# The first adaLN modulation of a two-layer diffusion block: plain fp32 weights in four column groups instead of split weights

## The chip, the cores and the metric

The kernel runs on one core of a Trainium2 chip. The metric is the device time of one execution in microseconds (us), as the median of several runs; lower is better. All tensors in HBM are fp32.

## The reference, cut to what matters

Two layers run over 256 latent tokens and 256 context tokens of width 1024. Every layer begins by turning the conditioning vectors `c` (latent) and `c_ctx` (context) into six modulation vectors each, and the first two of these shift and scale the normalised input of the token mixer:

```python
silu_c, silu_cc = jax.nn.silu(c), jax.nn.silu(c_ctx)
mod_lat = (silu_c @ w_mod[l] + b_mod[l])[:, None, :]      # w_mod[l]: 1024 x 6144
mod_ctx = silu_cc @ w_mod[l] + b_mod[l]
sh1, sc1, gt1, sh2, sc2, gt2 = jnp.split(mod_lat, 6, axis=-1)
h  = rms_norm(x,   g_pre_mix[l]) * (1.0 + sc1)  + sh1
hc = rms_norm(ctx, g_pre_mix[l]) * (1.0 + csc1) + csh1
... = jnp.split(h @ w_in[l], SPLIT_POINTS, axis=-1)       # w_in[l]: 1024 x 6912
```

The case is about the very first of these products, `sh1` and `sc1` of layer 0 for both streams, because nothing else can start on TensorE in earnest before them: `h` is needed by every later product of the layer.

## The kernel before, in words

Almost all products of the kernel are "split" products. A helper (`split`, L163; in the prologue `cut`, L252) writes a fp32 tile as the sum of two fp32r tiles, a high part (a cast on ScalarE) and a low part (a subtraction on VectorE). `mm3` (L178) then adds up three TensorE products: high by high, high by low, low by high. `mm3_pair` (L184) does the same for two independent products whose operands sit in different halves of the partitions, and issues the two alternately. Weights come from HBM in tiles of 512 KB (128 partitions x 1024 fp32).

**The prologue** (L233 to L355) computes `sh1` and `sc1` of layer 0, modulates the input, and does the first 512 columns of `w_in` (the retention's q and k). It works in four rounds `kp` of 256 channels. A round needs five weight tiles: four of `w_mod` (two vectors, and two halves `hf` of the contraction over 1024; each tile holds four blocks `k` of 128 rows, 256 columns wide) and one of `w_in`. The steps of a round have one letter each in `PLAN` (L54):

- `c`: `cut` up to tile n: high part on ScalarE, low part on VectorE. `cut` also calls `load`, so a transfer is issued on SP only `PLD` = 4 tiles ahead of the cutting.
- `a`: `mod` (L275): the stationary operand is `msr` (128 columns of which four are not zero: high and low part of silu(c) and of silu(c_ctx)), the moving operands are the high and the low weight tile. That makes 4 tiles x 4 blocks x 2 parts = 32 products of 256 columns, all into one PSUM tile `modps`.
- `r`: `row` (L286): ScalarE copies the four useful rows into `r5`, whose fifth row is the bias, brought by a transfer of its own (`bias`, L289).
- `t`: `pre_tr` (L500): TensorE transposes of the normalised input, eight of 128 columns for both streams, into `ph`.
- `f`: `fin` (L294): four plain fp32 products with a 5x2 selector turn the rows into columns `sh1`, `sc1` (PSUM tile `pm`, then three small VectorE instructions).
- `h`: `pre_h` (L509): four ScalarE instructions make h of both streams and two blocks of 128 channels, and VectorE splits each into `hT` (a cast and a subtraction).
- `g`: `gemm` (L306): 24 products of 512 columns into the four PSUM tiles `pr`.

While `Ordered.on` is true, VectorE, ScalarE and TensorE instructions keep the order of the program. Other instructions (transfers on POOL, splits of later weights, `setup2`) are put between them by the scheduler of the framework. `tc.issue_after(ins)` makes the instructions of a block follow `ins` on that instruction's own engine only. The last `gemm(3)` is issued after `Ordered.on` has been cleared.

Ahead of the prologue stands `setup` (L1264). Behind it `setup2` (L1275) brings the rope tables, the retention's decays and the gains by transfers on POOL, and computes decays on VectorE; it follows the last low part (`st["hold"]`) on VectorE. The following steps are the retention's v (`projB`, PSUM tile `pB`) and then the remaining projections, whose weights (`wr`, split into `wh` and `wl`) use three buffers each. The rest of the modulation is done on VectorE (`mod_dve`, L391) from `w_mod` rows that POOL brings (`mr`). The neighbourhood attention brings its bias tiles `bt` on POOL (L796).

The buffers: `sp` has `NS` = 31 tiles of 4 KB per partition (`S(...)`), used for X, weight tiles, `hT` and so on; `wrp`, `whp`, `wlp` have three each; PSUM has four banks `mm` and four banks `at`.

Of the kernel before, what the change touches and what calls it, by code (L numbers as in the profile page):

```python
# [9 lines left out]
F32 = mybir.dt.float32  # L10
# [23 lines left out]
C1 = 0  # L34
# [46 lines left out]
def kernel(  # L81
# [115 lines left out]
    cs = const.tile([128, 8, 2], F32, tag="cs", name="cs")  # L197
    brow = const.tile([128, 2, 512], F32, tag="brow", name="brow")
# [34 lines left out]
    def prologue():  # L233
        pr = []
        M = {}
        raw, rdy = {}, {}
# [3 lines left out]
        mi = (0, 5, 10, 15)  # L240
        gi = (4, 9, 14, 19)

        def load(n):
            while len(raw) < min(n, len(wts)):
                i = len(raw)
                ap, k, _, _ = wts[i]
                t = S("pr", F32) if i % RW else wrp.tile([128, 2, 512], F32, tag="wr", name="pr")
                raw[i] = t
                st["hold_sp"] = nc.sync.dma_start(
                    out=t.rearrange("p a b -> p (a b)").rearrange("p (k n) -> p k n", k=k), in_=ap)  # L250

        def cut(n):  # L252
            while len(rdy) < min(n, len(wts)):
# [7 lines left out]
                rdy[i] = [u.rearrange("p a b -> p (a b)").rearrange("p (k n) -> p k n", k=k) for u in (hi, lo)]  # L261

        def init():
            msr = S("msr")
            v_.tensor_copy(msr[:, 0, :], brow[:, 0, :])
            v_.tensor_copy(msr[:, 1, :], brow[:, 0, :])
            msr = msr.rearrange("p a b -> p (a b)").rearrange("p (k m) -> p k m", k=8)
            v_.tensor_copy(msr[:, :, 0:2], cs)
            tt(msr[:, :, 2:4], cs, f(msr[:, :, 0:2]), ALU.subtract)
            M["msr"] = msr  # L270
# [18 lines left out]
        def bias(kp):  # L289
            r5 = st["r5", kp] = T("r5")  # L290
            nc.gpsimd.dma_start(out=r5[4:5, :].rearrange("o (v n) -> o v n", v=2),
                                in_=b_mod[0:1, 0:2 * D].rearrange("o (v n) -> o v n", v=2)[:, :, 256 * kp:256 * kp + 256])

        def fin(kp):  # L294
            r5 = st.pop(("r5", kp))
# [10 lines left out]
        def gemm(kp):  # L306
            w_ = rdy[gi[kp]]
# [6 lines left out]
        def go(ws):  # L314
            Ordered.on = True
            load_x(4)
            load(PLD)
            for kp in range(2):
                bias(kp)
# [4 lines left out]
            cut(C1)  # L324
            pre_xn(1, sq[1])
            for kp, plan in enumerate(PLAN):
                for c in plan.replace("_", " ").split():
                    o, n = c[0], int(c[1:])
                    if o == "c":
                        cut(n)  # L330
                    elif o == "a":
                        mod(n)
                    elif o == "r":
                        row(n)
                    elif o == "t":
                        ph = [pre_tr(n, s) for s in range(2)]
                    elif o == "f":
                        fin(n)
                        if n < 2:
                            bias(n + 2)  # L340
                    elif o == "h":
                        h32 = [T("h32") for _ in range(2)]
                        for j in range(2):
                            for s in range(2):
                                pre_h(0, 0, n, s, ph[s], (j,), h32[s])
# [1147 lines left out]
```

## Time and profile before

| | us |
|---|---|
| runs (device time) | 1476.2, 1478.07, 1477.75 |
| median | 1477.75 |
| the profiled execution's own time | 1477.88 |
| its span on the core (first to last instruction) | 1476.1 |
| time around the span | 1.78 |

The profile names instructions by engine (PE is TensorE's matmul, PEld its weight load, DVE is VectorE, ACT is ScalarE, POOL is GpSimd, SP is the sync engine whose queue issues most transfers), by line and by the names of the tiles written and read. Because of the `Ordered` wrapper almost every compute instruction has line 72, so the tile names tell them apart. A row of a timeline merges equal neighbours; its first number is the start in us from the beginning of the span, its second the length, and the bracket at the end tells how long the engine had been idle and what it had waited for. Matmul records overlap, because a record includes the pipeline's fill and drain; the pace is read from the start of one to the start of the next, or from a piece of the chain divided by its count.

### The profile page before, as it was taken

What the parts mean: (1) busy time and instruction counts of PE and PEld (TensorE: products, weight loads), DVE (VectorE), ACT (ScalarE), POOL (GpSimd) and SP (SyncE); (2) the same over time, 40 slices, a digit from 0 to 9 for tenths busy, and PEclk for the clock granted to TensorE, in tenths of its full rate; (3) what the DMA queues carried; (4) which work ended last, traced back from release to release, by engine and by line L of the source; (5) the groups of instructions that cost most, each with busy time, mean ns of one, the idle gap of its engine ahead of it and who ended that gap; (6) DMA issues with size and microseconds to landing.
All of it is one profiled execution on the core that took longest, in us unless ns stands there. A gap on an engine that the chain in (4) does not pass through costs nothing.

```text
span 1476.1 us, 20910 instructions
## 1 busy us (share of the span) xinstructions
PE 1427.8 (97%) x7926; PEld 1210.6 (82%) x7926; DVE 1079.2 (73%) x1999; ACT 746.6 (51%) x1259; POOL 68.1 (5%) x131
## 2 busy tenths in 40 slices
PE   4999999999999999999999999999999999799997
PEld 3878788877788888988878887788889999699886
DVE  5785687777998759977756546986877887667544
ACT  5563465555333447724335145664556665477542
POOL 2000000000110000100001101000000000000000
PEclk9999899999999999999999999999999999899999
DMA  8622122222566555746447547443223446378653
GB/s 290 193 73 72 43 58 71 63 87 80 167 178 188 166 199 172 239 148 213 157 129 228 169 130 242 145 129 101 72 86 106 145 140 187 113 210 251 209 185 116
DMA packets 231958, 219.64 MB, mean 149 GB/s; under 512 B 7653, under 2 KB 188957, under 8 KB 231857
## 3 DMA queue, kind: packets, MB, share of 16 engines
q1 hardware_dynamic: 217856, 170.42, 37.7%
q0 software_dynamic: 14000, 47.88, 10.7%
q8 instruction: 62, 1.02, 0.3%
q14 instruction: 40, 0.32, 0.1%
HBM read 217.22 MB, written 1.05 MB: 148 GB/s over the span
## 4 chain that ended last, share of the span: by engine, by line
PE 78%; issue 12%; DMA 4%; DVE 4%; ACT 1%; SPq 0%; POOL 0%; DVEq 0%; ACTq 0%; POOLq 0%
PE ps L72 33%; PE pO L72 20%; PE pB L72 6%; PE br L72 5%; DMA mr<-in_w_mod_dram 2%; PE po L72 2%; PE pt L72 2%; PE pr L72 2%; PE sl L72 2%; PE gkv L72 1%; PE modps L72 1%; DMA pr<-in_w_mod_dram 1%; PE ro L72 1%; DVE wl L72 1%; DVE acc L72 1%
## 5 line engine op out<-in xcount | busy, mean ns | idle before, releaser
L72 PE MATMUL ps<-hT,wh 128*128 128x256 f32 (+1 forms) x2480 | 602.5, 334 | 1.5 <-ACT wh L72 1.5
L72 ACT CAST wh<-wr 128x1024 fp32r<-128x1024 f32 x295 | 309.5, 1052 | 443.7 <-PE pO L72 175.9
L72 DVE TENSOR_TENSOR wl<-wr,wh 128x1024 fp32r<-128x1024 f32 x295 | 359.4, 1221 | 206.2 <-ACT wh L72 205.6
L72 PEld LDWEIGHTS ps<-hT,wh 128*128 128x128 f32 x2480 | 417.4, 189 | 54.5 <-issue 6.9
L72 PE MATMUL ps<-hT,wl 128*128 128x256 f32 (+1 forms) x1240 | 413.3, 333 | 2.2 <-DVE wl L72 2.2
L72 PEld LDWEIGHTS ps<-hT,wl 128*128 128x128 f32 x1240 | 233.8, 189 | 26.5 <-DVE wl L72 3.5
L72 PE MATMUL pO<-wh,u 128*128 128x512 f32 x768 | 243.4, 396 | 0.0
L72 PEld LDWEIGHTS pO<-wh,u 128*128 128x128 f32 x768 | 144.2, 188 | 34.7
L72 DVE SCALAR_TENSOR_TENSOR acc<-mr,cs,acc 128x1024 f32<-128x1024 f32 x112 | 141.1, 1280 | 30.1 <-DMA mr<-in_w_mod_dram 29.5
L72 PE MATMUL pO<-wl,u 128*128 128x512 f32 x384 | 152.0, 396 | 1.2 <-DVE wl L72 1.2
L72 PEld LDWEIGHTS pO<-wl,u 128*128 128x128 f32 x384 | 72.1, 188 | 18.9 <-DVE wl L72 1.6
L72 PE MATMUL pB<-wh,hT 128*128 128x512 f32 x256 | 83.6, 396 | 0.0
L448 POOL DMA_DIRECT2D mr<-in_w_mod_dram x80 | 43.0, 537 | 647.6 <-DVE acc L72 609.6
L72 PE MATMUL pO<-wh,yT 128*128 128x512 f32 x192 | 60.7, 395 | 0.0
L72 PEld LDWEIGHTS pB<-wh,hT 128*128 128x128 f32 x256 | 48.0, 187 | 11.2
L72 DVE TENSOR_TENSOR PT<-pt,PT 128x512 fp32r<-128x512 f32 x80 | 51.4, 681 | 2.9 <-ACT PT L72 2.3
L72 PE MATMUL pB<-wl,hT 128*128 128x512 f32 x128 | 50.5, 394 | 0.0
L72 ACT CAST PT<-pt 128x512 fp32r<-128x512 f32 x80 | 43.2, 600 | 8.6 <-PE pt L72 6.7
L72 PEld LDWEIGHTS pO<-wh,yT 128*128 128x128 f32 x192 | 35.9, 188 | 8.6
L72 PE MATMUL pt<-ident,P 128*128 128x128 f32 x320 | 42.0, 273 | 0.7 <-DVE P L72 0.5
L72 DVE TENSOR_TENSOR u<-rl,u 128x256 fp32r<-128x256 f32 (+1 forms) x71 | 36.6, 516 | 7.6 <-ACT u L72 7.5
L72 DVE TENSOR_SCALAR P<-P,su 128x512 f32<-128x512 f32 (+1 forms) x96 | 40.2, 439 | 1.6
(261 smaller groups left out, 1901.9 us busy)
## 6 DMA issues: line engine op xcount, KB each, us to landing
wr<-in_w_m_dram SPq DMA_DIRECT2D x143, 512.0 KB, 4.6
wr<-in_w_in_dram SPq DMA_DIRECT2D x104, 512.0 KB, 3.8
mr<-in_w_mod_dram POOLq DMA_DIRECT2D x80, 512.0 KB, 4.5
wr<-in_w_br_dram SPq DMA_DIRECT2D x24, 512.0 KB, 3.5
wr<-in_w_out_dram SPq DMA_DIRECT2D x24, 512.0 KB, 4.1
pr<-in_w_mod_dram SPq DMA_DIRECT2D x16, 512.0 KB, 7.0
bt<-in_relb_dram POOLq DMA_DIRECT2D x16, 192.0 KB, 2.8
X<-in_x_dram SPq DMA_DIRECT2D x4, 512.0 KB, 5.2
```

The source lines that it names most:

```text
L72: ins = call(*a, **k)
L448: nc.gpsimd.dma_start(out=w, in_=w_mod[l, 128 * kc:128 * kc + 128, vec * D:vec * D + D].rearrange("p (a n) -> p a n", a=2))
```

## The change

The four weight tiles of `w_mod` of a round are no longer split. Their fp32 tiles are moving operands as they come from HBM. The stationary operand is `csz`: for each of the eight blocks of the contraction 32 columns, of which two hold silu(c) and silu(c_ctx) in plain fp32 and thirty are zero. Block `k` of a tile writes the 32 PSUM partitions `32k` to `32k+31`, so four partial sums stand side by side; only `hf` accumulates. `row` is now a VectorE addition of the PSUM tile and a bias tile that is zero but for rows 0 and 1, and `fin` multiplies all 128 rows with a 128x2 selector `selp` that adds the four groups. Only the four `w_in` tiles are still split, by `cast` (`c`, ScalarE) and `cut` (`d`, VectorE). All 20 loads are issued at once (17 into `sp` tiles, three into `wrp`). When the 15th (`GATE` = 14) has landed, a small POOL copy into `late` runs; the transfers of `setup2`, `mr` and `bt` follow that copy on POOL. The list of the steps is new.

```diff
-C1 = 0
-RW = 2
-PLD = 4
-PLAN = ["c4 t0 a0 c5 r0 f0 h0 c9 g0 c13",
-        "a1 t1 r1 c14 f1 h1 c18",
-        "a2 r2 c19 g1 t2 f2 h2",
-        "a3 t3 r3 c20 f3 h3 g2"]
+PLAN = "t0 a0 c0 r0 f0 d0 h0 g0 a1 r1 t1 c1 f1 d1 h1 a2 r2 t2 g1 c2 f2 d2 h2 a3 r3 t3 g2 c3 f3 d3 h3"
+GATE = 14
...
-        def load(n):
-            while len(raw) < min(n, len(wts)):
-                i = len(raw)
-                ap, k, _, _ = wts[i]
-                t = S("pr", F32) if i % RW else wrp.tile([128, 2, 512], F32, tag="wr", name="pr")
+        def load():
+            for i, (ap, k, _, _) in enumerate(wts):
+                t = wrp.tile([128, 2, 512], F32, tag="wr", name="pr") if i % 5 == 4 and i < 15 else S("pr", F32)
                 raw[i] = t
-                st["hold_sp"] = nc.sync.dma_start(
-                    out=t.rearrange("p a b -> p (a b)").rearrange("p (k n) -> p k n", k=k), in_=ap)
-
-        def cut(n):
-            while len(rdy) < min(n, len(wts)):
-                i = len(rdy)
-                load(i + PLD)
-                t, k = raw[i], wts[i][1]
-                hi = whp.tile([128, 2, 512], F32R, tag="wh", name="pwh") if i % 3 == 0 else S("pwh")
-                lo = wlp.tile([128, 2, 512], F32R, tag="wl", name="pwl") if i % 3 == 0 else S("pwl")
-                st["hold_act"] = s_.copy(hi, t)
-                st["hold"] = tt(lo, t, f(hi), ALU.subtract)
...
+                st["hold_sp"] = nc.sync.dma_start(out=flat(t, k), in_=ap)
+                if i == GATE:
+
+                    st["late"] = nc.gpsimd.tensor_copy(out=late, in_=t[:, 0, 0:1])
+
+        def cast(kp):
+            hi[kp] = whp.tile([128, 2, 512], F32R, tag="wh", name="pwh")
+            st["hold_act"] = s_.copy(hi[kp], raw[5 * kp + 4])
+
+        def cut(kp):
+            lo = wlp.tile([128, 2, 512], F32R, tag="wl", name="pwl")
+            st["hold"] = tt(lo, raw[5 * kp + 4], f(hi[kp]), ALU.subtract)
+            rdy[kp] = [flat(u, 2) for u in (hi[kp], lo)]

         def init():
...
+            M["bias"] = [S("bias", F32) for _ in range(2)]
+            for i, t in enumerate(M["bias"]):
+                v_.memset(t, 0.0)
+                for kp in range(2):
+                    c = 512 * i + 256 * kp
+                    nc.gpsimd.dma_start(
+                        out=t[0:2, kp, :].rearrange("o (v n) -> o v n", v=2),
+                        in_=b_mod[0, 0:2 * D].partition_broadcast(2).rearrange("o (v n) -> o v n", v=2)[:, :, c:c + 256])
+            v_.memset(selp, 0.0)
+            for j in range(4):
+                r = slice(32 * j, 32 * j + 2)
+                v_.tensor_copy(selp[r, :], ident[r, r])
...
         def mod(kp):
-            ps = att("modps")
+            ps = M["ps", kp] = att("modps")
             for i in range(4):
                 v, hf = i // 2, i % 2
-                w = rdy[mi[kp] + i]
+                w = flat(raw[5 * kp + i], 4)
                 for k in range(4):
-                    for p in range(2):
-                        t_.matmul(ps[:, 256 * v:256 * v + 256], M["msr"][:, 4 * hf + k, :], w[p][:, k, :],
-                                  start=(hf == 0 and k == 0 and p == 0), stop=(hf == 1 and k == 3 and p == 1))
-            M["ps", kp] = ps
+                    t_.matmul(ps[32 * k:32 * k + 32, 256 * v:256 * v + 256], csz[:, 4 * hf + k, :], w[:, k, :],
+                              start=(hf == 0), stop=(hf == 1))

         def row(kp):
-            s_.copy(st["r5", kp][0:4, :], M["ps", kp][0:4, :])
...
+            r = M["r", kp] = T("r5")
+            tt(r, M["ps", kp], M["bias"][kp // 2][:, kp % 2, :], ALU.add)
...
-                t_.matmul(pt[:, 2 * j:2 * j + 2], r5[0:5, 128 * j:128 * j + 128], sel[0:5, 18:20],
-                          start=True, stop=True)
+                t_.matmul(pt[:, 2 * j:2 * j + 2], r[:, 128 * j:128 * j + 128], selp, start=True, stop=True)
...
             gemm(3)
-            with tc.issue_after(st["hold"].ins):
+            with tc.issue_after(st["hold"].ins), tc.issue_after(st["late"].ins):
                 setup2()
...
-                nc.gpsimd.dma_start(
-                    out=w, in_=w_mod[l, 128 * kc:128 * kc + 128, vec * D:vec * D + D].rearrange("p (a n) -> p a n", a=2))
...
+                with tc.issue_after(st["late"].ins):
+                    nc.gpsimd.dma_start(
+                        out=w, in_=w_mod[l, 128 * kc:128 * kc + 128, vec * D:vec * D + D].rearrange("p (a n) -> p a n", a=2))
...
-                        nc.gpsimd.dma_start(out=bt, in_=relb[l, h])
+                        with tc.issue_after(st["late"].ins):
+                            nc.gpsimd.dma_start(out=bt, in_=relb[l, h])
...
+        v_.memset(csz, 0.0)
+        v_.tensor_copy(csz[:, :, 0:2], cs)
```

## Rows read from the trace of the kernel before

**Rows 1.** The page: TensorE's share, and the chain that ended last by engine.

```profile
PE 1427.8 (97%) x7926; PEld 1210.6 (82%) x7926; DVE 1079.2 (73%) x1999; ACT 746.6 (51%) x1259; POOL 68.1 (5%) x131
...
PE 78%; issue 12%; DMA 4%; DVE 4%; ACT 1%; SPq 0%; POOL 0%; DVEq 0%; ACTq 0%; POOLq 0%
```

**Rows 2.** Windows: us, busy PE, PEld, DVE, ACT, POOL, granted clock, DMA share, GB/s.

```profile
4.00:16.00 12.00, 1.38 (x4) 0.68 (x4) 5.41 (x33) 5.64 (x9) 6.37 (x12) 1.00 1.02 336
...
31.00:36.00 5.00, 5.00 (x12) 3.86 (x13) 4.93 (x9) 5.00 (x7) 0.00 (x0) 0.50 0.45 154
...
40.00:74.00 34.00, 34.00 (x215) 30.31 (x214) 25.48 (x74) 18.67 (x30) 1.01 (x2) 1.00 0.56 175
```

**Rows 3.** The chain in order of time, 0 to 76 us: start, length, what.

```profile
4.13 16.13 DMA pr<-in_w_mod_dram
...
22.64 4.57 PE modps L72 x23
...
27.86 1.06 PE pm L72 x8
...
30.82 8.37 PE pr L72 x24
39.19 3.78 PE modps L72 x32
42.97 0.87 PE ph L72 x8
43.84 0.98 PE pm L72 x8
...
48.80 5.51 PE pr L72 x24
...
61.96 11.12 PE pr L72 x48
```

**Rows 4.** ScalarE's timeline: its waits for transfers, 8 to 26 us.

```profile
8.65 1.06 ACT L72 ACTIVATE xj<-X 128x1024 f32<-128x1024 f32 x1 [0.28 <-DMA X<-in_xc_dram]
...
12.75 1.06 ACT L72 ACTIVATE xj<-X 128x1024 f32<-128x1024 f32 x1 [2.95 <-DMA X<-in_xc_dram]
...
20.28 1.04 ACT L72 CAST pwh<-pr 128x1024 fp32r<-128x1024 f32 x1 [4.85 <-DMA pr<-in_w_mod_dram]
...
24.66 1.05 ACT L72 CAST pwh<-pr 128x1024 fp32r<-128x1024 f32 x1 [0.34 <-DMA pr<-in_w_in_dram]
```

**Rows 5.** POOL's timeline: issues of `setup2`, `mr`, and a wait.

```profile
4.60 0.55 POOL L1276 DMA_DIRECT2D lgt<-in_decay_dram  x1
...
12.06 0.54 POOL L448 DMA_DIRECT2D mr<-in_w_mod_dram  x1 [1.00 <-DMA lgt<-in_decay_dram]
...
63.96 0.50 POOL L451 DMA_DIRECT2D brow<-in_b_mod_dram  x1 [50.63 <-DVE lgp L72]
64.49 0.50 POOL L1282 DMA_DIRECT2D sel<-in_sel_dram  x1
```

**Rows 6.** Groups by tile and shape, 0 to 75 us: busy us, mean ns.

```profile
L72 DVE TENSOR_TENSOR pwl<-pr,pwh 128x1024 fp32r<-128x1024 f32 x20 | 23.5, 1219 | 8.6 <-ACT pwh L72 8.6
...
L72 PE MATMUL pm<-sel,r 5*128 5x2 f32 x32 | 4.2, 249 | 0.7 <-ACT r L72 0.7
```

**Rows 7.** VectorE's timeline: rows at 8.4, 13.9, 29.0 and 94.8 us.

```profile
8.41 0.17 DVE L72 TENSOR_SCALAR pv<-pms 128x2 f32<-128x2 f32 x1 [4.09 <-ACT xj L72]
...
13.93 0.17 DVE L72 TENSOR_SCALAR pv<-pms 128x2 f32<-128x2 f32 x1 [2.33 <-ACT xj L72]
...
28.95 0.16 DVE L72 COPY sh<-pm 128x4 f32<-128x4 f32 x1 [1.98 <-PE pm L72]
...
94.75 0.69 DVE L72 TENSOR_TENSOR rv<-pB,rv 128x512 fp32r<-128x512 f32 x1 [0.71 <-ACT rv L72]
```

**Rows 8.** TensorE's timeline: the first product of the modulation.

```profile
17.73 0.56 PE L72 MATMUL modps<-pwh,msr 128*128 128x256 f32 x1
```

**Rows 9.** TensorE's timeline, 101.0 to 101.8 us: a pair of row halves.

```profile
101.02 0.98 PE L72 MATMUL ra<-rq,rk 64*128 64x256 f32 x12
```

More of the change, by code (lines that the diff above doesn't have):

```diff
@@ L197 @@
     cs = const.tile([128, 8, 2], F32, tag="cs", name="cs")
+    csz = const.tile([128, 8, 32], F32, tag="csz", name="csz")
+    selp = const.tile([128, 2], F32, tag="selp", name="selp")
+    late = const.tile([128, 1], F32, tag="late", name="late")
     brow = const.tile([128, 2, 512], F32, tag="brow", name="brow")
@@ L235, in prologue @@
         M = {}
-        raw, rdy = {}, {}
+        raw, hi, rdy = {}, {}, {}
         md = lambda kp: [wspec(w_mod[0], 512 * hf, 4, v * D + 256 * kp, 256) for v in range(2) for hf in range(2)]
@@ L252, in cut @@
-        def cut(n):
-            while len(rdy) < min(n, len(wts)):
-                i = len(rdy)
-                load(i + PLD)
-                t, k = raw[i], wts[i][1]
-                hi = whp.tile([128, 2, 512], F32R, tag="wh", name="pwh") if i % 3 == 0 else S("pwh")
-                lo = wlp.tile([128, 2, 512], F32R, tag="wl", name="pwl") if i % 3 == 0 else S("pwl")
-                st["hold_act"] = s_.copy(hi, t)
-                st["hold"] = tt(lo, t, f(hi), ALU.subtract)
-                rdy[i] = [u.rearrange("p a b -> p (a b)").rearrange("p (k n) -> p k n", k=k) for u in (hi, lo)]
@@ L263, in init @@
-        def init():
[L264 to L270, printed above, removed]
+        flat = lambda t, k: t.rearrange("p a b -> p (a b)").rearrange("p (k n) -> p k n", k=k)
+        def load():
+            for i, (ap, k, _, _) in enumerate(wts):
+                t = wrp.tile([128, 2, 512], F32, tag="wr", name="pr") if i % 5 == 4 and i < 15 else S("pr", F32)
+                raw[i] = t
+                st["hold_sp"] = nc.sync.dma_start(out=flat(t, k), in_=ap)
+                if i == GATE:
+                    st["late"] = nc.gpsimd.tensor_copy(out=late, in_=t[:, 0, 0:1])
@@ L275, in mod @@
         def mod(kp):
-            ps = att("modps")
+            ps = M["ps", kp] = att("modps")
             for i in range(4):
                 v, hf = i // 2, i % 2
-                w = rdy[mi[kp] + i]
+                w = flat(raw[5 * kp + i], 4)
                 for k in range(4):
-                    for p in range(2):
-                        t_.matmul(ps[:, 256 * v:256 * v + 256], M["msr"][:, 4 * hf + k, :], w[p][:, k, :],
-                                  start=(hf == 0 and k == 0 and p == 0), stop=(hf == 1 and k == 3 and p == 1))
-            M["ps", kp] = ps
+                    t_.matmul(ps[32 * k:32 * k + 32, 256 * v:256 * v + 256], csz[:, 4 * hf + k, :], w[:, k, :],
+                              start=(hf == 0), stop=(hf == 1))
         def row(kp):
-            s_.copy(st["r5", kp][0:4, :], M["ps", kp][0:4, :])
[L289 to L292, printed above, removed]
+            r = M["r", kp] = T("r5")
+            tt(r, M["ps", kp], M["bias"][kp // 2][:, kp % 2, :], ALU.add)
         def fin(kp):
-            r5 = st.pop(("r5", kp))
+            r = M.pop(("r", kp))
             pt = att("pm")
             for j in range(4):
-                t_.matmul(pt[:, 2 * j:2 * j + 2], r5[0:5, 128 * j:128 * j + 128], sel[0:5, 18:20],
-                          start=True, stop=True)
+                t_.matmul(pt[:, 2 * j:2 * j + 2], r[:, 128 * j:128 * j + 128], selp, start=True, stop=True)
             p3 = pt[:, 0:8].rearrange("p (j e) -> p j e", e=2)
@@ L306, in gemm @@
         def gemm(kp):
-            w_ = rdy[gi[kp]]
+            w_ = rdy[kp]
             for k in range(2):
@@ L316, in go @@
             load_x(4)
-            load(PLD)
-            for kp in range(2):
-                bias(kp)
+            load()
             init()
@@ L323, in go @@
             sq.append(pre_sq(1))
-            cut(C1)
             pre_xn(1, sq[1])
[L326 to L345, printed above, removed]
-                    elif o == "g":
-                        gemm(n)
+            ph = {}
+            for c in PLAN.split():
+                o, n = c[0], int(c[1:])
+                if o == "c":
+                    cast(n)
+                elif o == "d":
+                    cut(n)
+                elif o == "a":
+                    mod(n)
+                elif o == "r":
+                    row(n)
+                elif o == "t":
+                    ph[n] = [pre_tr(n, s) for s in range(2)]
+                elif o == "f":
+                    fin(n)
+                elif o == "h":
+                    h32 = [T("h32") for _ in range(2)]
+                    for j in range(2):
+                        for s in range(2):
+                            pre_h(0, 0, n, s, ph[n][s], (j,), h32[s])
+                elif o == "g":
+                    gemm(n)
             Ordered.on = False
             gemm(3)
-            with tc.issue_after(st["hold"].ins):
+            with tc.issue_after(st["hold"].ins), tc.issue_after(st["late"].ins):
                 setup2()
@@ L447, in go @@
                 w = mrp.tile([128, 2, 512], F32, tag="mr", name="mr")
-                nc.gpsimd.dma_start(
-                    out=w, in_=w_mod[l, 128 * kc:128 * kc + 128, vec * D:vec * D + D].rearrange("p (a n) -> p a n", a=2))
-                if kc == 0:
-                    nc.gpsimd.dma_start(out=brow[0:1], in_=b_mod[l:l + 1, vec * D:vec * D + D].rearrange("o (a n) -> o a n", a=2))
+                with tc.issue_after(st["late"].ins):
+                    nc.gpsimd.dma_start(
+                        out=w, in_=w_mod[l, 128 * kc:128 * kc + 128, vec * D:vec * D + D].rearrange("p (a n) -> p a n", a=2))
+                    if kc == 0:
+                        nc.gpsimd.dma_start(out=brow[0:1], in_=b_mod[l:l + 1, vec * D:vec * D + D].rearrange("o (a n) -> o a n", a=2))
                 for s in streams:
```

2 lines of the change are left out of this document (removed).

## The prediction

> **What bounds the kernel now.** I read the page first: TensorE has work on it for 97% of the span and holds 78% of the chain that ended last [rows 1]. A change is therefore worth what it does to TensorE's own sequence: it shortens it, or it removes a wait in it. The change touches only the prologue, so I went on to the windows of the first 74 us [rows 2]. There are two stages. Up to about 26 us the transfers rule: TensorE works 1.4 of 12 us between 4 and 16 us while the DMA engines are full (share 1.02, 336 GB/s). From 31 us on TensorE is busy in every microsecond of the windows shown. The chain in order of time says the same [rows 3]: one transfer of w_mod until 20.26, then `modps` to 27.21, the finish of round 0, and from 30.82 to 73.08 matmul pieces with no gap. So what counts is when the first of the four `gemm` pieces starts (30.82), what stands on TensorE from there to 73.08, and whether a new gap appears.
>
> Two further readings. First, the pace. At full clock the 32 products of 256 columns take 3.78 us, 0.118 each, and 24 of 512 columns 5.51 us, 0.23 each [rows 3]. Between 31 and 36 us the granted clock is 0.50, that is 1.2 instead of 2.4 GHz, and 12 products take 5 us [rows 2]; TensorE had waited 1.9 us before [rows 3]. The 23 products from 22.64 on took 4.57 us, which is about 18 at half pace and five at full pace: the clock rose near 26.3, after some 3.7 us of these products. Second, the transfers. Weight tiles land one after another: three steps from 20.28 to 24.66, 1.46 us each [rows 4]. But the fourth X tile came 4.1 us after the third [rows 4], because POOL's transfers ran then [rows 5].
>
> **The change, part by part.** *Removed:* 16 of the 20 splits, each a cast on ScalarE and 1.22 us on VectorE [rows 6], and 128 products of 256 columns. After 31 us the splits lie beside gapless matmuls, so there their removal is worth nothing. In round 0 it is worth something, as part of an earlier start:
>
> - X. Without POOL's transfers beside it the fourth X tile lands one step after the third: 8.65 + 1.46 = 10.1 instead of 12.75. The statistics of the context stream then could start at 11.3 (13.93 is 1.18 behind 12.75), but the latent stream's, from 8.41, hold VectorE about 3.2 us (13.93 to 17.73 less 0.6 of transposes) [rows 7, 8]; so 11.65, which is 2.3 us earlier. TensorE is through with the transposes at 17.73 - 2.3 = 15.4.
> - The weights. The four tiles of round 0 follow X directly: 10.1 + 4 x 1.46 = 15.9, instead of 23.2 (one step before 24.66) [rows 4]. The 15th lands at 32, the 20th at 39 if nothing else runs; POOL's 1.9 MB behind the gate (the sizes of those tensors) add at most 6 us at 336 GB/s. Round 3 wants them after 50, so the gate itself costs and gains nothing; without that cover it would be those 6 us. The loads wait for no buffer: 4 X, 17 weight and 2 bias tiles leave 8 of 31, as many as `hT` needs.
>
> *Added, the new products:* 16 per round. Plain fp32 products leave two records each (32 `pm` records for 16 products in the code) [rows 6], so a round has 32 records of 256 columns. No row shows what such a record costs over many columns. Lower end: 0.118, one stream of 256 columns. Upper end: 0.228, the row of 512 columns, if it streams its columns twice. I take 0.228: `mm3` needs three split products and still drops low by low, so two records that keep all four must hold two each. A page of the Trainium skill, FP8 and Floating Point Precision, TensorE Precision Notes, states four passes for true fp32; a product would by it cost four times 0.118, an estimate of 0.47 that moves the sum by 0.4 us.
>
> *How far the four groups overlap.* No row shows column groups; the nearest is the pair of row halves: twelve products of 256 columns within 0.98 us [rows 9], where one after another would be 12 x 0.118 + 0.16 = 1.58. So products in different parts of the array do run side by side, and there the code issues the halves alternately. In `mod` it does not: the two records of a product are neighbours in the same 32 columns. If starts keep the program's order, the second record waits for the first, and the next group can start only beside the second. Then two of four groups overlap, and 16 products take 17 steps of 0.228 = 3.9 us, against 3.8 now. Ends: 1.8 us (all four side by side) and 7.3 (none).
>
> The Trainium skill bears on this: TensorE: Matmul & The Clock Gate, Part 3, says that matmuls start and end in program order and only weight loads move ahead. By that rule the sum is the one above; by its own table for column tiles (three in 2.38 times less time) one would expect nearer 1.8 us. The pair of row halves agrees with an overlap and does not test the order.
>
> *The sum.* `a0` from 15.4: I take the 3.7 us at half pace over from the row as they stand; they are 8.1 steps, the other 8.9 take 2.0, so 21.1 instead of 27.21. From there to `gemm(0)` it was 3.6 us [rows 3]. The row is now added on VectorE, 0.69 [rows 7] for a ScalarE copy that fitted into 0.65 with its waits: +0.1. The low part `d0` (1.22) now stands on VectorE between `fin` and h; about half of it lies in the time in which VectorE, behind its row at 28.95 [rows 7], waits for the first h anyway: +0.55. `gemm(0)` starts at 21.1 + 4.3 = 25.4, and I leave its 8.37 us, since TensorE again has waited before it: 33.8. Rounds 1 to 3 up to the last finish: three modulations 11.7, transposes 3 x 0.87, finishes 3 x 0.98, two gemms of 5.51 [rows 3]; together 28.3, which is what they take now (39.19 to 67.5). So 62.1. Here is a new wait: before, `gemm(2)` stood behind the last finish and hid h; in the new list the last finish comes after `gemm(2)`, so `gemm(3)` waits for h as in round 0: 1.9 + 0.55, and 0.6 for half a chance of a later weight's split (1.22) between them: 3.05. `gemm(3)` ends at 65.1 + 5.5 = 70.6 instead of 73.08: 2.5 us gained. Everything behind is TensorE's chain and moves along.
>
> Small things at nothing: two memsets of 128x1024 (a pass over such a tile is 1.22 at most [rows 6]) fall into VectorE's 4.09 us of idle time before 8.41 [rows 7]; without it they would delay the statistics by 2.4. Changes between whole-array and column-group products, eight in all: 0 to 0.1 each, taken as 0, kept in the range. Bias transfers are four as before. On SP the later weights (`wr`) now queue behind all 20 loads, so they are issued from about 39 on and wanted at 70. Behind the POOL copy are queued `setup2`, `bt` and `mr`, issued between 4.6 and 12.6 today [rows 5]; the rope tables among them are wanted at 70, some 25 us after they land.
>
> The profiled execution took 1477.88, its span 1476.1; the sum is 1477.88 - 2.5 = 1475.4, and the median of the runs stands 0.13 below the profiled one: 1475.3.
>
> **The rivals.** *All four groups side by side* (or a record streams once and two overlap): 1.8 us per round, 3.65 at half pace. `a0` ends at 19.05, `gemm(0)` at 31.7, the last finish at 53.8, and 0.6 is lost as `a` covers less of h: `gemm(3)` ends at 63.0, 10.1 gained: 1467.7. For it: the row halves [rows 9]; against: the order of the records.
>
> *The column groups do not overlap*: 7.3 us per round. `a0` ends at 24.5 and each later round adds 3.4, so 13.7 on the forecast: 1489.0, slower. It decides from 4.5 us per round on, where the 2.5 us are used up. For it: no row shows such groups, and here each product reads all 128 partitions, while the row halves read 64 each. Against: the same row.
>
> *The bias rows come late.* POOL works in order, and the copy waits for the 15th tile. If the scheduler puts the bias transfers behind it, `r0` starts at 33 instead of 21.1 even if they land at once: 1487. For it: on this queue a transfer of `sel4` stood 50 us behind one that waited for VectorE [rows 5]. Against: today it issues what is ready first.
>
> *It does not do what it says*: transfers that start no earlier because SP's queue is full anyway. Then `a0` would end near 27 as today and the new wait would remain: 1481. The fourth X tile, late only while POOL's transfers ran, speaks against it; it is most of the 0.05 below.
>
> **How the numbers follow.** The forecast has 0.50, the overlap of four 0.25, no overlap 0.13, late bias rows 0.07; 0.05 is for the last rival and for what I have not thought of. About 0.2%, 3.0 us, can be told from no change. The forecast's own range is 1472 to 1479: the clock in `gemm(0)` is worth up to 2.7, the last wait 1.2, the group changes 0.8. Of its chance 0.22 lies below 1474.8. So faster 0.25 + 0.22 = 0.47, the same 0.28, slower 0.25. The range is 1466.5 to 1486.0; it holds the first two cases and leaves out most of the slow ones, 0.2.
>
> **What would show it.** Right: `gemm(0)` starts near 25, `modps` pieces of 3.9 us from round 1 on, pairs of records with nearly one start, TensorE idle some 3 us before the last 24 `pr` products, which end near 70.6. Wrong: `modps` pieces of 2 or 7 us; a wait of the addition for the bias transfer; TensorE waiting for the tiles of round 3; a stall behind 73 us that takes the gain back, such as rope waiting for its tables.

## The result, and the profile after

The changed kernel takes 1498.36 us in the median of four runs, against 1477.91 for the kernel before in the same comparison: a ratio of 1.014, with a 95% interval of 1.0117 to 1.0162. It is 20 us slower, where 2.5 us faster were forecast, and 12 us beyond the upper end of the range. The profiled execution took 1498.14 with a span of 1496.4.

The first lines of the page after, TensorE's busy time and the chain by engine, beside [rows 1]:

```profile
PE 1423.3 (95%) x7926; PEld 1201.9 (80%) x7926; DVE 1064.4 (71%) x1992; ACT 728.9 (49%) x1239; POOL 67.9 (5%) x132
...
PE 87%; DVE 5%; DMA 4%; ACT 1%; SPq 1%; issue 1%; DVEq 0%; POOL 0%; ACTq 0%; POOLq 0%
```

TensorE works 4.5 us less than before in a span that is 20 us longer. So it waits, and the question is where. The windows of the changed kernel (columns as in [rows 2]):

```profile
4.00:16.00 12.00, 3.79 (x20) 1.96 (x24) 8.18 (x39) 4.73 (x9) 0.00 (x0) 1.00 1.05 392
18.50:42.00 23.50, 0.00 (x0) 0.00 (x0) 0.33 (x1) 0.00 (x0) 7.14 (x14) 0.56 0.98 362
```

Up to 16 us it is ahead of before. Then, for 23.5 us, TensorE and ScalarE do nothing at all and VectorE next to nothing, while the transfers run on. The chain in order of time, which answers to [rows 3], shows what they wait for:

```profile
20.96 8.37 DMA pr<-in_w_in_dram
29.33 0.05 issue
29.39 0.18 POOL late L250
29.57 0.46 POOL lgt L1273
30.03 5.01 DMA cosT<-in_cos_dram
35.08 0.66 issue
35.74 5.83 DMA bias<-in_b_mod_dram
41.67 0.70 DVE r L67
42.42 1.88 PE pm L67 x8
...
46.67 8.34 PE pr L67 x24
55.01 1.86 PE modps L67 x32
...
76.58 0.80 PE pm L67 x8
...
79.75 7.21 PE pr L67 x24
86.95 5.13 PE pB L67 x22
```

The addition `r` needs the bias rows; they come from POOL's queue; and there the copy `late` stands ahead of them, which waits for the 15th weight tile. The last `pr` product ends at 86.95 instead of 73.08. POOL's own timeline, beside [rows 5]:

```profile
29.39 0.18 POOL L250 COPY late<-pr 128x1 f32<-128x1 f32 x1 [26.39 <-DMA pr<-in_w_in_dram]
29.50 0.54 POOL L1273 DMA_DIRECT2D lgt<-in_decay_dram  x1
30.03 0.54 POOL L1274 DMA_DIRECT2D cosT<-in_cos_dram  x1
...
33.19 0.54 POOL L442 DMA_DIRECT2D mr<-in_w_mod_dram  x1
34.36 0.54 POOL L442 DMA_DIRECT2D mr<-in_w_mod_dram  x1 [0.63 <-DMA lgt<-in_decay_dram]
35.74 1.16 POOL L267 DMA_DIRECT2D bias<-in_b_mod_dram  x2 [0.85 <-DMA cosT<-in_cos_dram]
```

The bias rows are behind the copy and behind nine further transfers. And the ninth of these and the first bias transfer each wait for the landing of the transfer eight places ahead of them (`lgt` for `mr`, `cosT` for the first bias row). In the trace POOL's transfers report their landings on eight semaphores in turn, and a transfer waits for the semaphore that it takes over. So the price is not only the copy: the first bias transfer is issued 6.35 us behind it, and its landing takes 5.83 more.

The loss of 13.9 us at the end of the `pr` products is not the whole 20. I compared the start of the nth matmul record in the two profiles: from 213 to 1328 us of before the changed kernel is 12.3 to 11.4 us late, from 1375 us on 20.2. The waits between 1322 and 1400 us (who <- whom: us in total, times, longest) have two rows that before hasn't in this size:

```profile
DVE acc L67 <- DMA mr<-in_w_mod_dram: 8.2, 5, 4.3
...
PE ps L67 <- DVE wl L67: 5.4, 3, 4.5
POOL mr L442 <- DVE wl L67: 4.6, 1, 4.6
```

In before the first two are 2.5 (longest 1.2) and 0.8 (longest 0.6). The wait of TensorE is not all of it. Behind it the granted clock falls (same columns as above):

```profile
1359.50:1366.20 6.70, 5.18 (x24) 5.19 (x25) 4.74 (x7) 2.45 (x5) 0.00 (x0) 0.50 0.49 136
```

In before it is 1.00 all the way from 1310 to 1400 us. Of the 8.4 us lost here, 4.6 are the longer waits of TensorE (5.4 less 0.8), and some 3.4, an estimate, are 6.8 us of work at half clock. The change doesn't touch this place, a modulation row of layer 1 on VectorE, woven into the MLP. So there were two losses to explain.

### The profile page after: what moved, and what is told of

Read it like the earlier page. It is cut to its first block, busy times and chain, and to the rows that moved or that the text cites. A ratio compares the mean times of both kernels' runs of the same rounds, so it can differ in the third digit from the quotient of the medians.

```text
span 1496.4 us, 20871 instructions
## 1 busy us (share of the span) xinstructions
PE 1423.3 (95%) x7926; PEld 1201.9 (80%) x7926; DVE 1064.4 (71%) x1992; ACT 728.9 (49%) x1239; POOL 67.9 (5%) x132
## 4 chain that ended last, share of the span: by engine, by line
PE 87%; DVE 5%; DMA 4%; ACT 1%; SPq 1%; issue 1%; DVEq 0%; POOL 0%; ACTq 0%; POOLq 0%
PE ps L67 39%; PE pO L67 21%; PE br L67 6%; PE pB L67 6%; PE po L67 3%; PE pt L67 2%; PE sl L67 2%; PE pr L67 2%; DMA mr<-in_w_mod_dram 1%; PE gkv L67 1%; DMA wr<-in_w_m_dram 1%; SPq L247 1%; DVE wl L67 1%; PE ro L67 1%; PE ph L67 1%
## 5 line engine op out<-in xcount | busy, mean ns | idle before, releaser
L67 ACT ACTIVATE h<-ph,sh,sc 128x256 f32<-128x256 f32 x56 | 26.8, 573 | 54.1 <-DVE sc L67 46.0
```

Source lines behind the costliest of these rows:

```text
L67: ins = call(*a, **k)
```

## The experiments

Each run is set against the kernel before on the same chip, as a ratio with its 95% interval. "Late loss" is how much the nth matmul record falls back against before's profile between 1328 and 1375 us. It and the end of `pr` come from one profiled execution each.

| kernel | median us | ratio, 95% | `pr` ends | late loss |
|---|---|---|---|---|
| before | 1478 | 1 | 73.08 | 0 |
| changed | 1498.36 | 1.0140 (1.0117 to 1.0162) | 86.95 | 8.4 |
| e1_bias_first | 1475.57 | 0.9980 (0.9962 to 0.9998) | 64.35 | 8.8 |
| e2_no_gate | 1481.78 | 1.0033 (1.0019 to 1.0047) | 69.28 | 10.1 |
| e3_no_groups | 1495.51 | 1.0117 (1.0097 to 1.0138) | 83.83 | 10.1 |
| e4_bias_f3 | 1475.49 | 0.9986 (0.9968 to 1.0003) | 60.04 | 8.4 |
| e5_bias_nogate | 1477.66 | 0.9993 (0.9978 to 1.0007) | 68.80 | 9.4 |
| e6_before_plus1 | 1479.10 | 1.0005 (0.9988 to 1.0022) | 72.16 | 2.6 |
| e7_bias_sp | 1469.59 | 0.9935 (0.9913 to 0.9958) | 59.98 | 4.9 |
| e8_replan | 1460.88 | 0.9872 (0.9850 to 0.9895) | 53.73 | 1.8 |
| e9_before_dma1 | 1481.85 | 1.0033 (1.0017 to 1.0050) | 73.86 | 7.4 |
| e10_half_desc | 1471.68 | 0.9953 (0.9934 to 0.9972) | 63.09 | 5.2 |
| e11_late_half | 1496.07 | 1.0113 (1.0082 to 1.0144) | 87.30 | 3.2 |
| e12_replan_nogate | 1468.55 | 0.9929 (0.9902 to 0.9955) | 62.08 | 1.9 |

A caution on single profiles: e6 and e9 run the prologue of before unchanged, yet between 167 and 213 us both gain some 6 us on before's profile. The granted clock accounts for it: before's profile has it at 0.50 from 169.6 to 183.2 us, those two have it so for 3.4 us or not at all. A profiled execution can also be far from the median: e4's took 1469.76, e10's 1476.19. Differences of that size in one pair of profiles are not read as effects below, unless several kernels show them.

**The bias rows first.** The bias tiles and transfers are made ahead of the loads, and the copy is issued behind them:

```diff
             load_x(4)
+            binit()
             load()
             init()
...
+                    with ExitStack() as es:
+                        for i_ in range(4):
+                            es.enter_context(tc.issue_after(M["bi", i_ // 2, i_ % 2].ins))
-                    st["late"] = nc.gpsimd.tensor_copy(out=late, in_=t[:, 0, 0:1])
+                        st["late"] = nc.gpsimd.tensor_copy(out=late, in_=t[:, 0, 0:1])
```

> The changed kernel with the four bias transfers put ahead of the copy on POOL; nothing else is moved. Theory (the bias rows queued behind that copy are the loss): the first r no longer waits until 41.67 us but runs when modps is done, at about 18.5 us; gemm(0) starts at about 23.5 us instead of 46.67; the last pr product ends at about 64 us instead of 86.95 (73.08 in the kernel before), and the span comes to about 1467 us, 9 below before; if the second loss of some 8.5 us near 1340 to 1375 us comes back it is about 1476 instead. Rival (the weights, or POOL's other transfers, would have set the rounds anyway): r moves forward but the rounds wait for pr tiles, pr ends after 75 us, and the time stays above before's.

The chain of this kernel, in order of time:

```profile
18.73 0.70 DVE r L67
...
23.72 8.56 PE pr L67 x24
32.28 1.86 PE modps L67 x32
...
53.85 0.80 PE pm L67 x8
...
57.02 7.33 PE pr L67 x24
64.35 22.40 PE pB L67 x96
```

`r` runs at 18.73, `gemm(0)` starts at 23.72 and `pr` ends at 64.35: the three numbers of the theory. The median falls by 22.8 us against the changed kernel. The second loss stayed, and with it the total is where the expectation put it in that case, 1476. So the place of four small transfers in POOL's queue costs more than the whole difference of 20 us, and the second loss is another matter.

**No gate.** The changed kernel without the copy and without the three waits on it:

```diff
-                if i == GATE:
-
-                    st["late"] = nc.gpsimd.tensor_copy(out=late, in_=t[:, 0, 0:1])
...
-                with tc.issue_after(st["late"].ins):
+                if True:
```

> The changed kernel without the copy on POOL and without the waits on it, so all of POOL's transfers go out as early as they can, with the bias rows still behind nine of them. Theory (the copy's place ahead of the bias rows is the loss, the gate itself protects little): the bias rows are issued between 14 and 19 us and landed by 24, r at about 25, gemm(0) at about 29, pr ends at about 70 us, and the weights of round 0 land at most 3 us later than the 14.54 us of the changed kernel; total about 1473, or 1481 if the late loss near 1340 us stays. Rival (the gate is needed: without it POOL's transfers take the weights' bandwidth): the weights of round 0 land after 20 us, the 20th after 45, and pr ends after 78 us.

The first expectation held in the total: 16.6 us of the 20 go with the copy and its waits, and `pr` ends at 69.28. One part of it failed. The fourth weight tile lands at 22.70, 8.2 us later than in the changed kernel, where at most 3 had been expected. So the gate protects more than I gave it. POOL's transfers now run beside X and the first weights; the transposes of the context stream wait 4.81 us for X, and the first `modps` ends at 23.82 instead of 18.66 in e1. The bias rows have landed by 19.7 and `r` doesn't wait for them, so what separates e2 from e1 is the gate: 5 us in the profile and 6.2 in the medians.

**No column groups.** e1_bias_first with all sixteen products of a round in the first group (the addition and the finish then use its 32 rows alone):

```diff
-                    t_.matmul(ps[32 * k:32 * k + 32, 256 * v:256 * v + 256], csz[:, 4 * hf + k, :], w[:, k, :],
-                              start=(hf == 0), stop=(hf == 1))
+                    t_.matmul(ps[0:32, 256 * v:256 * v + 256], csz[:, 4 * hf + k, :], w[:, k, :],
+                              start=(hf == 0 and k == 0), stop=(hf == 1 and k == 3))
```

> e1_bias_first with the sixteen products of a round all in the first 32-column group, one after the other, instead of in four groups. Theory (the four groups run side by side): 32 records of modps take about 7.3 us at full pace (0.228 each, the two-stream price of the kernel before) instead of 1.86, so the four rounds give back some 20 us and pr ends at about 84 us. Rival (a record of 32 columns is simply short, the groups don't matter): a round stays at 1.9 us and the time is that of e1_bias_first.

Two pieces of its chain, the first at half pace until 19.2 us:

```profile
15.17 9.04 PE modps L67 x32
...
35.99 7.02 PE modps L67 x32
```

7.02 us against 1.86: a record takes 0.22 by itself, the two-stream price, and four groups divide it by 3.8. The whole gain of the changed kernel's modulation hangs on the groups; without them e1's 0.998 is 1.0117.

**The last finish ahead of gemm(2).** e1_bias_first with another order of the list:

```diff
-... a3 r3 t3 g2 c3 f3 d3 h3
+... a3 r3 t3 c3 f3 g2 d3 h3
```

> e1_bias_first with the last finish (pm, sh, sc, split, hT of round 3) put ahead of gemm(2) instead of behind it, as the rounds before it have it. Theory (the new wait of the predicted kind, 2.38 us idle plus a slow-clock start of the last gemm, is real and sits on the path): pr of gemm(3) starts right after gemm(2), pr ends 3 to 4 us earlier than in e1_bias_first, and the total is 3 to 4 us lower. Rival (the wait only moves: PE then waits for r ahead of gemm(2)): no difference above 1 us.

Inconclusive, nearer to the rival. From the start of `gemm(0)` to the end of `pr` the profile has 38.05 us instead of 40.63, but TensorE now waits 1.98 us for `r` ahead of `gemm(2)`, because `r` stands on VectorE behind the split and hT of round 2; and the medians are the same (1475.49 and 1475.57); the profiled execution of e4 is the fastest of its ten. The wait moved, in part at least.

**What the second loss is.** POOL's issue of the last `mr` and the last three `acc` rows in before, then in the changed kernel (two timelines each):

```profile
1336.98 0.53 POOL L448 DMA_DIRECT2D mr<-in_w_mod_dram  x1 [1.27 <-DVE acc L72]
...
1335.40 1.28 DVE L72 SCALAR_TENSOR_TENSOR acc<-mr,cs,acc 128x1024 f32<-128x1024 f32 x1 [0.52 <-DMA mr<-in_w_mod_dram]
...
1340.53 2.63 DVE L72 SCALAR_TENSOR_TENSOR acc<-mr,cs,acc 128x1024 f32<-128x1024 f32 x2
```

```profile
1352.53 0.53 POOL L442 DMA_DIRECT2D mr<-in_w_mod_dram  x1 [4.62 <-DVE wl L67]
...
1348.11 1.29 DVE L67 SCALAR_TENSOR_TENSOR acc<-mr,cs,acc 128x1024 f32<-128x1024 f32 x1 [1.02 <-DMA mr<-in_w_mod_dram]
...
1352.91 1.28 DVE L67 SCALAR_TENSOR_TENSOR acc<-mr,cs,acc 128x1024 f32<-128x1024 f32 x1 [0.31 <-DMA mr<-in_w_mod_dram]
...
1358.54 1.28 DVE L67 SCALAR_TENSOR_TENSOR acc<-mr,cs,acc 128x1024 f32<-128x1024 f32 x1 [4.34 <-DMA mr<-in_w_mod_dram]
...
1361.02 0.58 PE L67 MATMUL ps<-hT,wl 128*128 128x256 f32 x1 [4.50 <-DVE wl L67]
```

The transfer reuses the buffer of two steps earlier, so it waits for that step's `acc`. In before it is issued 0.30 us after that `acc` ends (1336.68), in the changed kernel 3.13 (after 1349.40). The row names `wl` as what it waited for, but in e1, e2 and e3 the delay ends at another place in VectorE's work and is still 2.83 to 2.84 longer than 0.30: it is a fixed time of POOL's, and VectorE's `wl` only happened to end there. What follows is plain: the last `acc` waits 4.34 us for its row, the splits behind it on VectorE are late, and TensorE waits 4.50. The computing instructions there and their order on each engine are the same in both kernels. Four runs looked for what puts the 2.83 us there.

First, by the length of POOL's program: e4 without the copy (what stood behind the copy now stands behind the last bias transfer), and before with one idle memset on POOL.

```diff
         nc.gpsimd.dma_start(out=sel, in_=sel_in)
+        nc.gpsimd.memset(idle, 0.0)
```

> e4_bias_f3 without the copy on POOL and without the waits on it (the bias transfers stay first). It serves two questions. First, the late loss: in the changed kernel and in e1 to e4 the last mr transfer of layer 1 is issued 2.83 to 2.84 us later after the acc instruction it waits for than in the kernel before, and some 8.5 us are lost behind it; POOL's program has 243 to 245 instructions in those five kernels and 242 in the kernel before and in this one. Theory L (the stall comes from POOL's own program, by its length): the 2.83 us are gone here, the offset against before does not change between 1310 and 1380 us, and the time is some 8 us below e4's 1475.5 as far as the gate is worth nothing. Rival (the stall comes from the moment at which the step runs, or from the weights' new order): it is there again. Second, the gate: if it protects the weights, the weights of round 0 land some 4 us later than with it and the transposes of X wait longer, as in e2; if it protects nothing, pr ends where e4's does.

> The kernel before with one more instruction on POOL, a memset of a 128x1 tile that nobody reads, behind its first three transfers (243 instructions instead of 242). Theory L (length of POOL's program): the last mr transfer is issued 2.8 us later after its acc than before, PE then waits near 1340 us, and the time rises by some 8 us to about 1486. Rival (the stall has to do with the first modulation or the moment of the step): no change, 1478 within 2 us.

Theory L fell twice: e5 has before's number of instructions and the stall (late loss 9.4), e6 has one more and no stall there (its last `mr` is issued 0.29 us after its `acc`). On its second question e5 says little: `pr` ends 8.8 us later in its profile, the medians differ by 2.2 and their intervals overlap.

Then the four bias transfers were taken off POOL and put on SP's queue behind the fifth weight tile, and, in e8, the list of steps was changed as well:

```diff
-                    nc.gpsimd.dma_start(
+                    M["bi", i, kp] = nc.sync.dma_start(
...
-PLAN = "t0 a0 c0 r0 f0 d0 h0 g0 a1 r1 t1 c1 f1 d1 h1 a2 r2 t2 g1 c2 f2 d2 h2 a3 r3 t3 g2 c3 f3 d3 h3"
+PLAN = "t0 a0 c0 r0 f0 a1 t1 d0 h0 r1 g0 c1 f1 d1 h1 a2 r2 t2 g1 c2 f2 d2 h2 a3 r3 t3 x2 c3 f3 d3 h3 y2"
```

(`x2` and `y2` are the two halves of `gemm(2)`; only e8 has the second change.)

> e4_bias_f3 with the four bias transfers on SP's queue behind the fifth weight tile instead of on POOL, the gate kept (POOL 239 instructions). Theory L: no 2.83 us stall, no loss between 1310 and 1380 us, and the whole gain of the first stage arrives at the end: about 1467 to 1468 us, 10 below before. Rival (moment of the step): 1475 as e4. The bias rows land before the first modps is done (18 us) in either case.

> e7_bias_sp with the rounds woven otherwise on TensorE: the products and transposes of round 1 fill the 2.4 us wait for the first hT ahead of gemm(0), and gemm(2) is cut in two halves with the last finish between them. Theory (the waits for hT at the first and the last round sit on the path, and the work moved into them is 1.9 + 1.0 us): pr ends 4 to 6 us earlier than in e7_bias_sp and the total is that much lower, about 1462 us if theory L holds. Rival (DVE sets the pace of a round: finish, split and hT take 5 us, r stands behind them, and the waits only move): within 1.5 us of e7_bias_sp.

e7 is 0.9935, 2 us short of what was expected. The stall at the last `mr` is gone; one of 2.8 us stands ahead of the second `gb` transfer (POOL is idle 5.08 us before it, against 2.27 in e4). So moving four transfers moved it by two places against e4, and that led to theory R: its place depends on how much POOL has transferred. In before it stands at the first `gb`: POOL's waiting instruction there ends at 1361.01 and the issue comes at 1364.37, 3.36 us later, against 0.50 at the same instruction of the changed kernel (1380.16 and 1380.67). Nobody waits for `gb` at that time, so before hides it.

e8 is the fastest kernel of the study: 1460.88 us, ratio 0.9872 (0.985 to 0.9895), faster than both. Its chain:

```profile
22.41 1.03 PE ph L67 x8
23.44 5.50 PE pr L67 x24
...
41.81 2.77 PE pr L67 x12
44.58 0.79 PE pm L67 x8
45.37 8.36 PE pr L67 x36
53.73 22.40 PE pB L67 x96
```

The products and transposes of round 1 now fill the wait for the first hT, `gemm(0)` takes 5.50 instead of 8.56 (e1), and the last finish lies between halves of `gemm(2)`, with no gap behind it. `pr` ends 6.3 us earlier than in e7 and the median is 8.7 lower. So the waits for hT did sit on the path; what e4 lacked was work to put into them. Part of this gain is the clock: in e7's profile the granted clock is 0.50 from 20.1 to 26.8 us and `gemm(0)` takes 8.07, in e8's it is 1.00 from 17.1 to 54 us. The two changes of the list were made together and are not told apart, and some of the 8.7 us come late (late loss 1.8 instead of 4.9).

**Pieces, not transfers or instructions.** Theory R was then tested on both kernels: one more transfer in before, and half the pieces at an equal number of transfers in e4.

```diff
         nc.gpsimd.dma_start(out=sel, in_=sel_in)
+        nc.gpsimd.dma_start(out=idle, in_=sel_in)
```

```diff
-                for kp in range(2):
-                    c = 512 * i + 256 * kp
+                for v in range(2):
+                    c = v * D + 512 * i
...
-                        out=t[0:2, kp, :].rearrange("o (v n) -> o v n", v=2),
-                        in_=b_mod[0, 0:2 * D].partition_broadcast(2).rearrange("o (v n) -> o v n", v=2)[:, :, c:c + 256])
+                        out=t[0:2, v, :],
+                        in_=b_mod[0, c:c + 512].partition_broadcast(2))
```

> The kernel before with one more transfer on POOL at its start: sel once more, 128 rows of 80 bytes, into a tile that nobody reads. Runs so far: the same stall of 2.83 us ahead of one of POOL's last transfers is in every kernel, but its place differs: at the first gb transfer in before and e6_before_plus1 (nobody is waiting for it there), one transfer earlier, at the last mr, in the changed kernel and e1, e4, e5 (four bias transfers of 2x2 rows on POOL in place of four of 1x2), and one later, at the second gb, in e7 and e8 (none of the four on POOL). An instruction more on POOL did not move it. Theory R (its place is set by how many pieces POOL's transfers have had since the start): one whole transfer more moves it by one, so here it comes at the last mr (issued 3.1 us after its acc instead of 0.3), PE waits near 1340 us, and the time rises by 5 to 9 us to about 1485. Rival (it belongs to the new modulation's weights or to the moment of the step): it stays at the first gb, and the time is 1478 within 2 us.

> e4_bias_f3 with the bias tile laid out so that each of the four bias transfers on POOL is two rows of 512 numbers instead of 2x2 rows of 256: half as many pieces, the same bytes, the same number of instructions. Theory R: the stall is no longer at the last mr but at the first gb as in before, nothing is lost between 1310 and 1380 us, and the time is 1467 to 1470 instead of e4's 1475.5. Rival (the number of transfers or instructions on POOL decides, or the moment of the step): the stall stays at the last mr and the time is e4's.

POOL's last issues and the waits behind them in e9:

```profile
1330.44 0.53 POOL L449 DMA_DIRECT2D mr<-in_w_mod_dram  x1 [4.05 <-DVE acc L72]
1335.05 0.54 POOL L449 DMA_DIRECT2D mr<-in_w_mod_dram  x1 [4.08 <-DVE wl L72]
...
1341.32 1.28 DVE L72 SCALAR_TENSOR_TENSOR acc<-mr,cs,acc 128x1024 f32<-128x1024 f32 x1 [4.54 <-DMA mr<-in_w_mod_dram]
...
1343.80 0.56 PE L72 MATMUL ps<-hT,wl 128*128 128x256 f32 x1 [4.79 <-DVE wl L72]
```

One idle transfer at 3 us puts the whole picture of the changed kernel into the kernel before, 1330 us later: the last `mr` is issued 3.16 us after its `acc` (1331.89), TensorE waits 4.79 us. The time rises by 3.5 us, less than the 5 to 9 expected. In e10 the last `mr` comes 0.29 us after its `acc` (1333.05), and the stall is back at the first `gb`, where POOL's waiting instruction ends at 1358.22:

```profile
1333.34 0.53 POOL L449 DMA_DIRECT2D mr<-in_w_mod_dram  x1 [3.82 <-DVE acc L67]
1361.59 1.09 POOL L411 DMA_DIRECT2D gb<-in_gpost_dram  x2 [27.71 <-PE ps L67]
```

Its ratio is 0.0033 below e4's, 4.9 us, with intervals that just meet, and its median is 3.8 us lower; 1467 to 1470 had been expected, 1471.7 was measured. The numbers of transfers, instructions and bytes are those of e4, so the layout of the four transfers decides. That it does so by the number of contiguous pieces is the reading that fits all kernels; the profile doesn't count pieces (it has 14000 packets on POOL's queue in before, e4 and e10 alike). Over the table, the late loss is 7.4 to 10.1 us in the seven kernels that have the stall at the last `mr`, and 1.8 to 5.2 in the six others beside before. It holds more than the stall: the granted clock is 0.50 for 6.8 us between 1310 and 1400 us in the changed kernel and e1 to e5, for 3.4 in e7, e9 and e10, and never in the other five. In the two medians the stall costs 3.5 (e9 against before) and 3.8 us (e4 against e10).

**Do the two losses add?** The last two runs: the changed kernel with the bias tile of e10 but the bias still behind the copy, and e8 without the gate.

> The changed kernel with the bias tile laid out so that each of the four bias transfers on POOL has two rows of 512 numbers instead of 2x2 rows of 256; they stay behind the copy. Theory (the two losses are separate and add: some 16 us for bias rows that come late, some 4 us for the stall of 2.83 us at the last mr): r still waits until about 41 us and pr still ends at about 87, the stall moves to the first gb, and the time is 1494 to 1495. Rival (the late loss is a consequence of the late start, since steps and weights meet in another phase): the time stays at 1498.

> e8_replan without the copy on POOL and without the waits on it: POOL's other transfers run beside the modulation's weights. Theory (the gate is worth what the weights of round 0 lose to those transfers: modps ended at 23.8 us in e2 and at 18.7 in e1): X and the weights of round 0 land 3 to 5 us later, pr ends 4 to 5 us later than in e8_replan, and the time is 1464 to 1466. Rival (the gate costs nothing and gives nothing, as the prediction had it): 1461 within 1.5 us.

e11: `r` at 41.70, `pr` ends at 87.30, and the late loss falls from 8.4 to 3.2. So in the profile the two losses are separate. In time it is not decided whether they add in full: the ratio falls from 1.014 to 1.0113, 4.0 us, but these two intervals overlap, and the median of 1496.07 lies between the 1494 to 1495 expected and the rival's 1498. e12 costs 7.7 us more than e8, twice what I expected: `pr` ends 8.35 us later, because not only the first `modps` (23.21 instead of 17.89) but also that of round 1, which e8 had moved into the gap, now runs at half pace and waits for its last tile:

```profile
24.26 1.86 PE L67 MATMUL pm<-selp,r 128*128 128x2 f32 x8 [1.05 <-DVE r L67]
26.05 2.82 PE L67 MATMUL modps<-pr,csz 128*32 128x256 f32 x24
29.15 1.08 PE L67 MATMUL modps<-pr,csz 128*32 128x256 f32 x8 [0.28 <-DMA pr<-in_w_mod_dram]
```

## Why the prediction was wrong

- **The step that failed: "Bias transfers are four as before."** I counted the transfers and not their place in the queue. What the gate does to POOL's order I had as a rival with a chance of 0.07, argued from `sel4` [rows 5] for it and from "it issues what is ready first" against. That the copy stands first in the order and cannot be passed was readable from the code; which transfers the scheduler puts between was not, and should have left the rival more than 0.07. Its price was also too low: `r` at 33 was put, 41.67 came, because nine transfers lie between, the ninth and the first bias transfer each wait for an earlier landing, and the bias row lands only 5.83 us after its issue. e1, with the same work and the bias first, is 22.8 us faster.
- **The sum without it was near, by luck.** e1's 1475.57 is the forecast's 1475.3, but by other steps. Two errors of opposite sign largely cancel:
   - *The overlap.* I took two of four groups, 3.9 us a round. All four run side by side: 1.86. The rival "all four groups side by side" was right in its size (1.8) and `pr` ends at 64.35 in e1 where it had 63.0. What I had against it, the order of the records, was no obstacle: in the changed kernel the records start in fours, within 0.02 us of each other (54.94 to 54.96), the next four 0.24 later and the further ones 0.22. The price of a record by itself, 0.228, was right (7.02 / 32 = 0.22), and so was 7.3 us without overlap. The table for column tiles in the Trainium skill, TensorE: Matmul & The Clock Gate, Part 3, had pointed nearer to 1.8: from its three tiles in 2.38 times less time one would put 3.2 times for four, an estimate, or 2.2 us. The 3.8-fold gain measured here is larger.
   - *The stall of POOL.* "A stall behind 73 us that takes the gain back" was on the list of what would prove me wrong, but not this one, and no row of before showed it as a cost: it stood where nobody waits. In e1's profile the late loss is 8.8 us, and the sum had nothing for it.
- **X and the weights.** The transposes end at 14.9 (15.4 forecast), the weights of round 0 are there by then, the first `modps` takes 3.43 us at half pace (3.65 in that rival). Right.
- **The gate "costs and gains nothing".** Wrong in both directions. It cost 23 us through the bias rows, and with these out of the way it is worth something: 7.7 us in e8's form, 6.2 between e1 and e2, while e4 and e5 can't be told apart. The 2.3 us that I credited to X's earlier landing are a part of that gain.
- **The new wait before gemm(3).** 3.05 forecast; the wait is 2.38, but the granted clock falls in it (0.89 in the mean of 74 to 90 us) and `gemm(3)` takes 7.21 instead of 5.51: 4.1 together. I had the clock in the sum for `gemm(0)` and forgot it here.
- **The range.** It ended at 1486 because the bias rival was priced at 1487. With the 8.7 us by which `r` was later than that, and 4 for the stall, it would have been 1499.7. That this is near 1498.36 is luck again: the rival still had 3.9 us a round, and by it `pr` would have ended at 91.0 instead of 86.95.

## What to carry to other kernels

When a wait is put on an in-order queue, list every instruction that the built program puts behind it, by name, and ask of each who needs it first; one small transfer there can cost more than the large ones that the wait was meant for. Where a change alters nothing but a wait's place, look also at what the wait frees: here `pr` ended 6.3 us earlier as soon as other work was moved into the gaps before hT. And where a second loss appears far from the edit, change one count at a time in both kernels until it moves: the instruction that the profile names as releaser was not the cause.

## What the hardware showed that was not expected

- Four 32-column groups of fp32 products run side by side: 32 records of 256 columns in 1.86 us, against 7.02 in one group, both at full clock.
- POOL stops once for about 2.8 us ahead of one of its last transfers. It stood at the first `gb`, at the last `mr`, one transfer earlier, or at the second `gb`, one later, and it moved with what POOL had transferred in the 1300 us before: four transfers of 2x2 pieces instead of 1x2 brought it one place earlier, one more transfer of 128 rows did the same, the four taken off POOL made it one place later, an instruction more did not move it. What POOL does in that time, the traces don't show.
- Behind a wait POOL's transfers go out eight at a time: each waits for the landing of the one eight places ahead (34.36 and 35.74 us in the changed kernel). This is a semaphore wait in the built program; that the chip asks for it, no run shows.
